# Two-layer trunk on one core: x parked in DRAM to give the weight ring a sixth place, shared-expert units spread over more blocks, and the second layer's gate and MoE conditioning summed on VectorE inside the delta rule's heads

## The chip, the cores and the metric

One core of a Trainium2 chip. The metric is device time in microseconds for one launch of the whole kernel; smaller is better. Engine names are those of the profile: PE is TensorE, DVE is VectorE, ACT is ScalarE, POOL is GpSimd, SP is SyncE, whose queue issues the weight loads.

## The reference

Input x is 512 positions by 1024 channels, float32. Two layers run over it. Each layer's six modulation vectors come from a conditioning vector c through a large matrix (`ada_w`, 1024 by 6144 per layer).

```python
cs = silu(c)
for i in range(2):
    mod = cs @ ada_w[i] + ada_b[i]
    sh1, sc1, gt1, sh2, sc2, gt2 = split(mod, 6)
    h = rmsnorm(x, norm_w[i, 0]) * (1 + sc1) + sh1
    y = short_conv_mixer(h, ...) if i == 0 else gated_deltanet_mixer(h, ...)
    x = x + gt1 * rmsnorm(y, norm_w[i, 1])
    h = rmsnorm(x, norm_w[i, 2]) * (1 + sc2) + sh2
    y = hier_moe(h, ...)
    x = x + gt2 * rmsnorm(y, norm_w[i, 3])
```

`short_conv_mixer` is a projection to three times the width, a causal convolution of three taps between two gates, and an output projection. `gated_deltanet_mixer` is linear attention with 8 heads of 128: a projection to q, k, v, z and two small columns (beta and decay) per head, a causal convolution of four taps, then per chunk of positions a triangular solve and a state update, a norm, a gate by z, and an output projection. `hier_moe` routes each of the 512 positions to 2 of 64 experts; each expert is 1024 to 256 (gate and up) and back (down), 3 MB of float32 weights. A shared expert with hidden width 512 runs over all positions.

## The kernel before

The kernel is written for one core, in the order mixer 0, MoE 0, mixer 1 (the delta rule), MoE 1.

**The ring.** All large weights pass through `load()` (lines 121 to 138). It takes a tile of 128 by 4096 floats (2 MB) from a pool of 5 buffers, and issues one DMA (L137) or two halves (L135) on SP's queue. SP's order is the order in which the code calls `load()`; a load waits until the instructions that read the old piece in its buffer are done. x itself lies in SBUF beside the ring, 16 KB of each partition, in the same size as one ring piece. At the end of each MoE x is also in SBUF for the residual addition.

**A MoE stage.** The experts are taken in 18 blocks, 14 of four experts' slots ("Q") and 4 of two ("P"), in the order of the string `ORDER`. A Q block needs four ring pieces of gate and up weights (`block_gu`) and two of down weights (`block_dn`). TensorE's order is written out by hand here: gate and up (L1322, PSUM tile `gu`), gather of the next blocks' rows (L1270), scatter of the block before (L1379, `sca`, added into `y` by VectorE at L1384), the down-projection (L1357, tile `po`; for the last block L1346, tile `pol`). In between come units of the shared expert: eight of `shared_up` (L1408) and four of `shared_down` (L1431), one unit at each Q block from 2 to 15, and two at block 16. Behind the last block's gate and up comes a loop for expert overflow (L1530), which does not run for this input, but in front of which every engine waits for the others and for all DMAs in flight. Then the last block's rows are scattered and, chunk by chunk, `finish_chunk` multiplies by the gate (`ft`, L1681 on VectorE and L1682 on GpSimd) and adds into x (L1686).

**The seam to layer 1.** The norm of the next layer follows (`norm_t`: transposes L333, output `ghi` and `glo`, L343 to L345), together with one group of the modulation.

**Modulation.** `ada_units(i, groups, ...)` makes one of three groups of `ada_w[i]` at a time: group 0 is shift and scale before the mixer, group 1 the mixer's gate and the MoE's shift, group 2 the MoE's scale and its gate. One group is four ring pieces. Two ways exist: `unit` multiplies on TensorE (16 matmul steps per piece, L271), and `unit_summed` forms the weighted sum over the 8 parts of the contraction on VectorE (`adasum`, L286 and L288), so that TensorE needs only a row (L216), four short sums (L292), and the finish (L216 gate, L230 columns). In the kernel before, three groups are summed on VectorE during mixer 0: groups 1 and 2 of layer 0 and group 0 of layer 1. Group 1 of layer 1 is made with `unit` at the seam, and group 2 with `unit` in head 7 of the delta rule.

**The delta rule.** The Tile scheduler sets the order of all engines but SP here. For each head a 2 MB piece `gdn_w` is split into a high and a low part (`whi` on ScalarE, L680, `wlo` on GpSimd, L681, in eighths with four buffers), and three matmuls per part and channel block (L383 to L385, tile `pj`, 96 a head) make q, k, v and z. These stand between the small steps of the head before: the matrix L of the chunk (`LT`), four Newton steps between TensorE and VectorE (`Tc`, `V`, `Uc`; L874 to L894), the larger blocks of the inverse (`W`, `T`, `U`; L906 to L929), and the state steps (`vn`, `S`; L945 to L959). Ahead of head 0 stand two columns per head from a small piece `gdn_ba` (tile `ba`, `beta`, the decay `gg` at L738).

## Time and profile before

| | us |
|---|---|
| runs of the kernel before | 1823.75, 1824.9, 1825.8; median 1824.9 |
| profiled execution, its own time | 1825.65 |
| its span on the device | 1823.8 |
| TensorE busy | 1616.1 (89%) |
| VectorE busy | 852.8 (47%) |
| ScalarE busy | 479.1 (26%) |
| GpSimd busy | 175.6 (10%) |
| HBM read | 517.11 MB, 286 GB/s over the span |

The stages lie in the span about as follows: mixer 0 until 204 us, output projection and the front of MoE 0 until 268, MoE 0 until 786, the seam until 830, the delta rule until 1233, output projection and front until 1283, MoE 1 until 1801, the last additions and stores until the end. The share of TensorE is an average over stages whose limits differ, so the tables by stage and the timeline at the seams say more than the page.

### The profile page before, as it was taken

To read this page: it belongs to the slowest core of one execution; us is meant where nothing else is said; L and a number is where in the kernel's file an instruction comes from. 1 tells how busy PE (TensorE), PEld (TensorE's weight loads), DVE (VectorE), ACT (ScalarE), POOL (GpSimd) and SP (SyncE) were. 2 spreads that over 40 slices of the span, in tenths; PEclk is the share of its full clock that TensorE was granted. 3 is DMA by queue.
4 is the path that set the end of the run, shared out by engine and by line. 5 is a ranking of instruction groups with operands and counts; after the bars stand their busy time and mean duration, and the time that the engine had idled before them with its cause. 6 is when DMAs were issued, how large, how long until landed. Compare 5 with 4: busy or idle time off the path is not lost. (4 is left out here: it accounts for less than half of the span.)

```text
span 1823.8 us, 27772 instructions
## 1 busy us (share of the span) xinstructions
PE 1616.1 (89%) x11102; PEld 985.6 (54%) x11102; DVE 852.8 (47%) x1761; ACT 479.1 (26%) x978; POOL 175.6 (10%) x160
## 2 busy tenths in 40 slices
PE   6999977899999998868998999998689999989985
PEld 3777755445445454426676766656444545445542
DVE  1886454434334342445666666625543424334335
ACT  4222351211111110034344434415231111111101
POOL 1000110000000000024323323310000000000001
PEclk8999987999999999988999999999699999999997
DMA  9873426999999999786111111116589999999992
GB/s 402 353 304 124 202 108 250 376 419 418 420 417 411 419 419 419 292 353 244 62 59 59 59 59 59 53 59 271 208 336 420 416 419 418 419 419 415 420 399 93
DMA packets 71511, 523.17 MB, mean 287 GB/s; under 512 B 8340, under 2 KB 8532, under 8 KB 16852
## 3 DMA queue, kind: packets, MB, share of 16 engines
q1 hardware_dynamic: 67684, 511.02, 68.6%
q10 hardware_dynamic: 3696, 10.34, 1.6%
q8 instruction: 89, 1.46, 0.3%
q14 instruction: 42, 0.34, 0.0%
HBM read 517.11 MB, written 4.23 MB: 286 GB/s over the span
## 5 line engine op out<-in xcount | busy, mean ns | idle before, releaser
L1384 DVE TENSOR_TENSOR y<-y,sca 128x512 f32<-128x512 f32 x272 | 186.0, 686 | 97.3 <-PE sca L1379 96.4
L1322 PE MATMUL gu<-ring,xTb 128*32 128x512 f32 (+1 forms) x1024 | 170.6, 634 | 31.8 <-DMA ring<-in_moe_gu 31.8
L1270 PE MATMUL gat<-ohg,ghi 128*128 128x256 f32 x576 | 162.6, 304 | 32.1 <-DVE ohg L1245 10.8
L1326 DVE TENSOR_TENSOR hid<-hid,gu 128x256 f32<-128x256 f32 x36 | 15.2, 421 | 311.0 <-ACT hid L1325 311.0
L1270 PE MATMUL gat<-ohg,glo 128*128 128x256 f32 x576 | 154.7, 291 | 0.0
L1270 PEld LDWEIGHTS gat<-ohg,ghi 128*128 128x128 f32 x576 | 113.8, 198 | 61.4 <-ACT xTb L1276 17.4
L1379 PE MATMUL sca<-ohi,G 128*128 128x512 f32 x288 | 126.4, 439 | 15.6 <-DVE y L1382 5.4
L1322 PE MATMUL gu<-ring,xTa 128*32 128x512 f32 (+1 forms) x1024 | 134.6, 610 | 0.2
L1322 PEld LDWEIGHTS gu<-ring,xTb 128*32 128x32 f32 (+1 forms) x1024 | 47.3, 119 | 147.1 <-issue 82.9
L1379 PE MATMUL sca<-olo,G 128*128 128x512 f32 x288 | 118.5, 411 | 0.0
L1270 PEld LDWEIGHTS gat<-ohg,glo 128*128 128x128 f32 x576 | 114.1, 198 | 7.9
L1357 PE MATMUL po<-ring,hT 128*32 128x512 f32 (+1 forms) x896 | 118.1, 602 | 0.0
L1682 POOL TENSOR_TENSOR ft<-y,gt 128x512 f32<-128x512 f32 x8 | 12.4, 1550 | 1058.9 <-DVE y L1384 1058.1
L1408 PE MATMUL mix<-h2T,shw 128*128 128x512 f32 x256 | 114.1, 599 | 0.0
L385 PE MATMUL pj<-ghi,wlo 128*128 128x512 f32 x264 | 113.4, 430 | 0.2 <-POOL wlo L681 0.2
L383 PE MATMUL pj<-ghi,whi 128*128 128x512 f32 x264 | 110.3, 418 | 1.6 <-DVE xh L789 0.8
L1325 ACT ACTIVATE hid<-gu 128x256 f32<-128x256 f32 x36 | 13.9, 385 | 357.8 <-PE gu L1322 357.8
L384 PE MATMUL pj<-glo,whi 128*128 128x512 f32 x264 | 107.8, 408 | 0.0
L681 POOL TENSOR_TENSOR wlo<-ring,whi 128x512 fp32r<-128x512 f32 x66 | 86.1, 1305 | 184.7 <-ACT whi L680 125.1
L1372 DVE SCALAR_TENSOR_TENSOR olo<-po,tab_s,ohi 128x512 fp32r<-128x512 f32 x68 | 51.1, 751 | 96.6 <-ACT ohi L1371 96.6
L1379 PEld LDWEIGHTS sca<-ohi,G 128*128 128x128 f32 x288 | 56.1, 195 | 62.8 <-issue 31.1
L1322 PEld LDWEIGHTS gu<-ring,xTa 128*32 128x32 f32 (+1 forms) x1024 | 36.6, 115 | 88.5 <-issue 88.2
(402 smaller groups left out, 2781.7 us busy)
## 6 DMA issues: line engine op xcount, KB each, us to landing
ring<-in_moe_gu SPq DMA_DIRECT2D x256, 1024.0 KB, 14.5
ring<-in_moe_w_down SPq DMA_DIRECT2D x120, 1024.0 KB, 13.2
ring<-in_ada_w SPq DMA_DIRECT2D x24, 2048.0 KB, 10.8
ring<-in_gdn_w SPq DMA_DIRECT2D x8, 2048.0 KB, 12.3
ring<-in_conv_in_w SPq DMA_DIRECT2D x8, 1536.0 KB, 11.8
shw<-in_shared_gu SPq DMA_DIRECT2D x16, 512.0 KB, 15.4
x<-in_x SPq DMA_DIRECT2D x8, 512.0 KB, 6.3
ring<-in_conv_out_w SPq DMA_DIRECT2D x2, 2048.0 KB
```

The source lines that it names most:

```text
L383: mm(out, ah, bh, start=first, stop=False)
L384: mm(out, ah, bl, start=False, stop=False)
L385: mm(out, al, bh, start=False, stop=last)
L681: nc.gpsimd.tensor_tensor(out=wlo, in0=w[:, k:k + 4], in1=r32(whi), op=ALU.subtract)
L1270: nc.tensor.matmul(g[:, kk], part[:, c, k], oh[:, c], start=(kk + c + lo == 0), stop=(kk + lo == 2 and c == TC - 1), skip_group_check=True)
L1322: nc.tensor.matmul(gu[s * j:s * j + s], xT[k][:, s * j:s * j + s], pieces(j, k), start=(k == 0), stop=(k == K - 1), skip_group_check=True)
L1326: nc.vector.tensor_tensor(out=hid, in0=hid, in1=gu[:, 256:512], op=ALU.mult)
L1357: self.nc.tensor.matmul(po[h][s * j:s * j + s], hT[:, k, s * j:s * j + s], pieces(j, k)[:, 512 * h:512 * h + 512], start=(k == 0), stop=(k ...
L1372: nc.vector.scalar_tensor_tensor(lo, po[h], gcol, r32(hi), op0=ALU.mult, op1=ALU.subtract)
L1379: nc.tensor.matmul(sc, G[:, c * P:(c + 1) * P], part, start=(n == 0), stop=(n == 1))
L1384: nc.vector.tensor_tensor(out=ys, in0=ys, in1=sc, op=ALU.add)
L1408: nc.tensor.matmul(acc, w[:, k], self.h2T[:, k], start=(k == 0), stop=(k == K - 1))
```

## The change

1. **Ring.** The pool of 5 buffers becomes a list of 5 named tiles, `self.pieces`, taken round robin (`ring_63` to `ring_67` in the listings below). At the start of a MoE stage x's own tile is appended to the list as a sixth place. For that, each chunk of x is written to a DRAM tile `xk` on ScalarE's queue as soon as the output projection has added into it. Behind the last block's weights, SP reads the four chunks back into x, ahead of the overflow loop.
2. **Units.** The table `UNITS` names the block of each of the 12 shared-expert units: 2, 3, 5, 5, 6, 8, 9, 9, 11, 12, 14, 15. Block 16 has none, and the gate rows move from block 16 to 15.
3. **Modulation.** Groups 1 and 2 of layer 1 are no longer made with `unit`, but summed on VectorE as 16 half-units (one 128x2048 operation each), two in each head of the program text. Their partial sum, rows and copy live in one ring piece that the list gives up (`held`), so the ring has four places during the delta rule. The next layer's norm now takes eight PSUM tiles at once. The second half of the output weights is loaded after the loop over k instead of before it.

```diff
+UNITS = (2, 3, 5, 5, 6, 8, 9, 9, 11, 12, 14, 15)
...
-            t = self.ring.tile([P, 4096], F32, name="ring")
+            t = self.pieces.pop(0)
+            self.pieces.append(t)
...
+            self.pieces = [ring.tile([P, 4096], F32, name="ring%d" % n) for n in range(5)]
...
+            self.xk = tc.dram_tile([T, D], F32, name="xk")
...
-        def unit_summed(g, q):
+        def unit_summed(g, q, kks=range(2)):
...
-            w = self.load(wv[g, q].rearrange("p (k n) -> p k n", k=2), [P, 2, 2048])
-            if q == 0:
-                part[g] = sb.tile([P, 2048], F32, name="adasum", bufs=2)
-            for kk in range(2):
+            if 0 in kks:
+                piece[0] = self.load(wv[g, q].rearrange("p (k n) -> p k n", k=2), [P, 2, 2048])
+            w = piece[0]
+            if q == 0 and 0 in kks:
+                part[g] = kept[0] if kept else sb.tile([P, 2048], F32, name="adasum", bufs=2)
+            for kk in kks:
...
+        if kept:
+            return [lambda g=g, q=q, kk=kk: unit_summed(g, q, [kk]) for g in groups for q in range(4) for kk in range(2)]
...
+                if front:
+                    nc.scalar.dma_start(out=self.xk[c * P:(c + 1) * P], in_=self.x[:, c])
...
+                if not self.only:
+                    held = self.pieces.pop(0)
+                    kept = held[:, :2048], held[:, 2048:2560], held[:, 2560:3072]
+                    units = self.ada_units(1, [1, 2], sb, ps2, ("ob", 1, "ob", 1), summed=True, kept=kept)
...
+                    units[2 * h]()
...
-                        if h == H - 1 and not self.only:
-                            if n == 0:
-                                wo = [self.load_out(A["gdn_out_w"], 0)]
-                                units = self.ada_units(1, [2], sb, ps2, ("ob", 1, "ob", 1, "kt", 2, "xh", 2))
-                            units[n]()
+                        if h == H - 1 and not self.only and n == 0:
+                            wo = [self.load_out(A["gdn_out_w"], 0)]
...
+                    units[2 * h + 1]()
...
+            if not self.only:
+                self.xplace = self.x.rearrange("p c d -> p (c d)")
+                self.pieces.append(self.xplace)
...
-                for f in self.ada_units(1, [1], sb, ps, ("gat", 1, "gat", 1, "", 0, "olo", 2), hs[:, 0]):
-                    f()
...
-            n = 2 if b == NB - 2 else int(ne == 4 and not last and b > 1)
+            n = UNITS.count(b)
...
-            if b == NB - 2:
+            if b == NB - 3:
                 gt = self.gate_rows(shw, ps, 1, ("shw", "mix"))
...
+        if not self.only:
+            self.pieces = [p for p in self.pieces if p is not self.xplace]
+            for c in range(TC):
+                nc.sync.dma_start(out=self.x[:, c], in_=self.xk[c * P:(c + 1) * P])
         po = self.down_last(ps, hT, ne, dn)
         self.overflow(i, m, rt, hs, sb, ps)
-        if i == 0 and not self.only:
-            nc.scalar.dma_start(out=hs[:, 0], in_=self.A["rows"][1])
```

Where the scheduler sets the order, the diff does not show what moves. Three places, each before and after. A row is an instruction in its engine's order: line, operation, output and input tiles, size, and in brackets the engines or DMA lanes on which it waits.

TensorE at the seam, the end of the next layer's norm before (`np` are its transposes, `adaacc`, `adagp` and `adacp` are group 1, `pj` the projection):

```order
L333 MATMUL np<-cst,h2T 128x128 [waits DVE_49]
L333 MATMUL np<-cst,h2T 128x128 x3
L271 MATMUL adaacc<-ring,cs 32x512 [waits DMAHW1_49]
L271 MATMUL adaacc<-ring,cs 32x512 x7
L216 MATMUL adagp<-hs,cst 128x512 [waits Activation_49]
L230 MATMUL adacp<-cst,md 64x2 [waits DVE_49]
L230 MATMUL adacp<-cst,md 64x2 x15
L383 MATMUL pj<-ghi,whi 128x512 [waits DVE_49,Activation_49,Pool_49]
```

The same place now:

```order
L345 MATMUL np<-cst,h2T 128x128 [waits Activation_49]
L345 MATMUL np<-cst,h2T 128x128 x4
L345 MATMUL npo<-cst,h2T 128x128 x2
L345 MATMUL np<-cst,h2T 128x128
L395 MATMUL pj<-ghi,whi 128x512 [waits DVE_49,Activation_49,Pool_49]
L396 MATMUL pj<-glo,whi 128x512
```

The weight matmuls, the gate and the columns have left; the projection follows the last transpose.

SP's queue from the end of MoE 0 on, before (`gdn_w` are the heads' projection weights, `ada_w` the modulation's):

```order
L137 DMA ring<-in_gdn_ba 128x1024
L137 DMA ring<-in_ada_w 128x4096 x3
L137 DMA ring<-in_ada_w 128x4096 [waits DMAHW1_49]
L137 DMA ring<-in_gdn_w 128x4096 [waits DMAHW3_49,PE_49]
L137 DMA ring<-in_gdn_w 128x4096 [waits DMAHW4_49,PE_49]
```

And now:

```order
L141 DMA ring_63<-in_gdn_ba 128x1024
L141 DMA ring_65<-in_gdn_w 128x4096
L141 DMA ring_66<-in_ada_w 128x4096
L141 DMA ring_67<-in_gdn_w 128x4096
L141 DMA ring_63<-in_ada_w 128x4096 [waits DMAHW2_49,Pool_49]
L141 DMA ring_65<-in_gdn_w 128x4096 [waits DMAHW5_49,DMAHW3_49,Pool_49]
L141 DMA ring_66<-in_ada_w 128x4096 [waits DMAHW4_49,DMAHW3_49,DVE_49]
L141 DMA ring_67<-in_gdn_w 128x4096 [waits DMAHW7_49,DMAHW5_49,Pool_49]
```

Pieces of `ada_w` and `gdn_w` alternate through all eight heads, over four places; a piece waits for GpSimd's split of an older `gdn_w` piece, or for VectorE's sum of an older `ada_w` piece.

VectorE in head 3's Newton steps, before:

```order
L872 TENSOR_TENSOR Uc<-Uc,gcst 128x128 [waits DVE_49]
L970 TENSOR_SCALAR so<-so 128x4 [waits DVE_49]
L843 TENSOR_TENSOR DT<-gr,gcst 128x512 [waits DMAHW5_49]
L874 STREAM_TRANSPOSE Tc<-Uc 128x128 [waits DVE_49]
L972 TENSOR_TENSOR so<-so,cf 128x4 [waits Pool_49]
L881 TENSOR_TENSOR V_7800<-iv,gcst 128x128 [waits PE_49]
```

And now (`ring_64` is the held piece with the partial sum):

```order
L894 TENSOR_TENSOR Uc<-Uc,gcst 128x128 [waits DVE_49]
L296 TENSOR_SCALAR ring_64<-ring_66,cs 128x2048 [waits DMAHW2_49,PE_49]
L896 STREAM_TRANSPOSE Tc<-Uc 128x128 [waits DVE_49]
L988 TENSOR_TENSOR so<-cf 128x4 [waits Activation_49]
L298 SCALAR_TENSOR_TENSOR ring_64<-ring_66,cs,ring_64 128x2048 [waits DVE_49]
L903 TENSOR_TENSOR V_7635<-iv,gcst 128x128 [waits PE_49]
```

The first two half-units of group 2 stand in the first Newton step, ahead of `Tc` and ahead of `V`; two more stand in the next one. On TensorE 57 `pj` matmuls stand between head 3's first and last Newton step where 28 stood before, and 69 instead of 48 stand ahead of the matmuls on the decay `gg`. Of the 16 half-units the scheduler puts two ahead of the norm's output, two around the copy `ba`, two ahead of head 0's L, two in head 0's last steps, four in head 3's Newton steps, two where head 3 passes to head 4, and two in head 4's last steps.

## Rows read from the trace of the kernel before

**Rows 1.** Engine busy by stretch: window; us; PE, PEld, DVE, ACT, POOL (count); PEclk, DMA share, GB/s

```profile
276.00:293.00 17.00, 13.00 (x66) 8.75 (x70) 6.88 (x28) 2.04 (x4) 0.00 (x0) 0.61 0.31 130
340.00:785.00 445.00, 409.21 (x2359) 207.13 (x2352) 157.18 (x281) 66.55 (x126) 0.00 (x0) 0.98 0.97 400
430.00:700.00 270.00, 254.27 (x1481) 129.67 (x1474) 99.12 (x173) 44.09 (x84) 0.00 (x0) 0.99 1.01 417
755.00:785.00 30.00, 24.28 (x142) 10.58 (x141) 7.32 (x13) 1.96 (x4) 0.00 (x0) 1.00 0.39 159
765.00:775.00 10.00, 9.33 (x54) 3.65 (x56) 5.14 (x8) 0.60 (x1) 0.00 (x0) 1.00 0.00 1
1770.00:1800.00 30.00, 24.77 (x132) 10.52 (x133) 7.46 (x13) 1.96 (x4) 0.00 (x0) 0.89 0.39 155
935.00:978.00 43.00, 40.07 (x488) 30.65 (x488) 28.20 (x76) 18.32 (x53) 14.49 (x12) 1.00 0.18 62
```

**Rows 2.** TensorE's groups by line, 340 to 785 and 1340 to 1801: busy, mean | idle before, releaser

```profile
L1322 PE MATMUL gu<-ring,xTb 128*32 128x512 f32 (+1 forms) x448 | 79.8, 659 | 15.6 <-DMA ring<-in_moe_gu 15.6
...
L1322 PE MATMUL gu<-ring,xTb 128*32 128x512 f32 (+1 forms) x448 | 76.3, 620 | 16.2 <-DMA ring<-in_moe_gu 16.2
```

**Rows 3.** TensorE's timeline, ends of both MoE stages: start, duration, operation [idle before <-releaser]

```profile
748.39 3.72 PE L1431 MATMUL sda<-shw,hs 128*128 128x256 f32 x16 [0.97 <-DVE y L1435]
...
782.17 3.62 PE L1346 MATMUL pol<-ring,hT 128*32 128x512 f32 x26 [0.99 <-DMA ring<-in_moe_w_down]
...
1797.54 3.62 PE L1346 MATMUL pol<-ring,hT 128*32 128x512 f32 x26 [0.92 <-DMA ring<-in_moe_w_down]
```

**Rows 4.** VectorE's timeline at the seam and ahead of head 0

```profile
794.83 0.69 DVE L1384 TENSOR_TENSOR y<-y,sca 128x512 f32<-128x512 f32 x1 [5.54 <-PE sca L1379]
...
840.49 0.23 DVE L715 COPY ba<-tp 128x64 f32<-128x64 f32 x1 [3.90 <-PE tp L712]
...
845.81 1.15 DVE L738 SCALAR_TENSOR_TENSOR gg<-xa,ea 128x32 f32<-128x32 f32 x1
```

**Rows 5.** TensorE's timeline, the projection's first matmul and two later ones

```profile
830.63 0.77 PE L383 MATMUL pj<-ghi,whi 128*128 128x512 f32 x1 [0.78 <-ACT whi L680]
...
842.12 0.40 PE L383 MATMUL pj<-ghi,whi 128*128 128x512 f32 x1
842.36 0.39 PE L384 MATMUL pj<-glo,whi 128*128 128x512 f32 x1
```

**Rows 6.** The tile adasum, its operations in mixer 0: count, duration in ns min/median/max

```profile
L288 DVE SCALAR_TENSOR_TENSOR adasum<-ring,cs,adasum x21: 2342/2349/2353, 50.3 to 152.1; 128x2048 f32<-128x2048 f32 x21
L286 DVE TENSOR_SCALAR adasum<-ring,cs x3: 1274/1282/1283, 49.0 to 120.3; 128x2048 f32<-128x2048 f32 x3
```

**Rows 7.** The page's DMA issues: count, KB each, us from issue to landing

```profile
ring<-in_gdn_w SPq DMA_DIRECT2D x8, 2048.0 KB, 12.3
```

**Rows 8.** GpSimd's timeline in head 0, the last eighth of a split

```profile
889.19 1.29 POOL L681 TENSOR_TENSOR wlo<-ring,whi 128x512 fp32r<-128x512 f32 x1 [3.32 <-PE pj L385]
```

**Rows 9.** VectorE's timeline in head 0's last steps

```profile
899.53 0.28 DVE L917 TENSOR_SCALAR T<-iv 32x128 f32<-32x128 f32 x1
...
904.85 0.35 DVE L950 TENSOR_SCALAR vn<-sc,cf 128x128 f32<-128x128 f32 x1 [0.95 <-PE sc L945]
```

**Rows 10.** TensorE's timeline, the finish of a summed group in mixer 0

```profile
156.58 1.12 PE L216 MATMUL adaacc<-rows,cst 4*128 4x512 f32 x2
157.63 1.06 PE L292 MATMUL adaacc<-adasum,cst 128*32 128x512 f32 x8
...
159.73 2.09 PE L230 MATMUL adacp<-cst,md 128*64 128x2 f32 x32
```

**Rows 11.** TensorE's groups by line in head 7, 1181 to 1199

```profile
L271 PE MATMUL adaacc<-ring,cs 128*32 128x512 f32 x64 | 10.7, 656 | 0.0
```

**Rows 12.** VectorE's timeline at the seam, the residual addition beside GpSimd's work and alone

```profile
802.87 2.32 DVE L1686 SCALAR_TENSOR_TENSOR x<-ft,fst,x 128x1024 f32<-128x1024 f32 x1
...
811.38 1.27 DVE L1686 SCALAR_TENSOR_TENSOR x<-ft,fst,x 128x1024 f32<-128x1024 f32 x1
```

More of the change, by code (lines that the diff above doesn't have):

```diff
@@ L41 @@
 NB = len(ORDER)
+UNITS = (2, 3, 5, 5, 6, 8, 9, 9, 11, 12, 14, 15)
+assert all(ORDER[b] == "Q" for b in UNITS)
 def block_ranks():
@@ L142, in run @@
         with tc.tile_pool(name="glob", bufs=1) as glob, \
-                tc.tile_pool(name="ring", bufs=5) as ring, \
+                tc.tile_pool(name="ring", bufs=1) as ring, \
                 tc.manual_schedule(engines={mybir.EngineType.SP}):
-            self.glob, self.ring = glob, ring
+            self.glob = glob
+            self.pieces = [ring.tile([P, 4096], F32, name="ring%d" % n) for n in range(5)]
             self.cst = glob.tile([P, C_END], F32, name="cst")
@@ L205, in ada_units @@
     def ada_units(self, i, groups, sb, ps, tags=("adaacc", 1, "adagp", 1, "adarow", 1, "adamd", 1),
-                  rows=None, queue=None, summed=False):
+                  queue=None, summed=False, kept=None):
         nc, A, m = self.nc, self.A, self.mods[i]
         wv = A["ada_w"][i]
-        if rows is None:
-            rows = sb.tile([P, 512], F32, tag=tags[4], name="rows", bufs=tags[5])
-            (queue or nc.scalar).dma_start(out=rows, in_=A["rows"][i])
+        rows = kept[1] if kept else sb.tile([P, 512], F32, tag=tags[4], name="rows", bufs=tags[5])
+        (queue or nc.scalar).dma_start(out=rows, in_=A["rows"][i])
         def row(g, acc, start):
@@ L219, in done @@
         def done(g, acc):
-            md = sb.tile([P, 512], F32, tag=tags[6], name="md", bufs=tags[7])
+            md = kept[2] if kept else sb.tile([P, 512], F32, tag=tags[6], name="md", bufs=tags[7])
             nc.scalar.activation(md, acc, AF.Copy)
@@ L288, in unit_summed @@
                     nc.vector.scalar_tensor_tensor(part[g], w[:, kk], c, part[g], op0=ALU.mult, op1=ALU.add)
-            if q == 3:
+            if q == 3 and 1 in kks:
                 place(g)
@@ L295, in unit_summed @@
                 done(g, acc[g])
-        part = {}
+        part, piece = {}, [None]
+        if kept:
+            return [lambda g=g, q=q, kk=kk: unit_summed(g, q, [kk]) for g in groups for q in range(4) for kk in range(2)]
         return [lambda g=g, q=q: (unit_summed if summed else unit)(g, q) for g in groups for q in range(4)]
@@ L767, in mixer1 @@
                 neg = gcst[:, C_NEG:C_NEG + P][:, None, :].to_broadcast([P, TC, P])
+                units = [lambda: None] * 16
+                if not self.only:
+                    held = self.pieces.pop(0)
+                    kept = held[:, :2048], held[:, 2048:2560], held[:, 2560:3072]
+                    units = self.ada_units(1, [1, 2], sb, ps2, ("ob", 1, "ob", 1), summed=True, kept=kept)
                 Uf = [sb.tile([P, TC, P], F32, name="U%d" % n) for n in range(2)]
@@ L982, in mixer1 @@
                     wo = [self.load_out(A["gdn_out_w"], 0)]
-                wo.append(self.load_out(A["gdn_out_w"], 1))
+                else:
+                    self.pieces.append(held)
                 sums = {c: ps.tile([P, T], F32, tag=("pj", "pj", "tp", "gq")[c], name="oacc", bufs=2 if c < 2 else 1)
@@ L994, in mixer1 @@
                         self.mm3(sums[c], yhi[:, c, k], ylo[:, c, k], whi, wlo, k == 0, k == K - 1)
+                wo.append(self.load_out(A["gdn_out_w"], 1))
             self.project_out(A["gdn_out_w"], 1, begun=(wo, sums))
@@ L1502, in moe @@
                 m1 = self.mods[1]
-                place = ["gu", "gu", "sca", "sca", "mix"]
+                place = ["gu", "gu", "sca", "sca", "mix", "", "", "gat"]
                 po = ps.tile([P, 2, T], F32, tag="po", name="npo", bufs=1)
@@ L1508, in tile_ps @@
                         return po[:, k - 5]
-                    tag = place[k % 7]
-                    return ps.tile([P, T], F32, tag=tag, name="np", bufs=1 if tag == "mix" else 2)
+                    return ps.tile([P, T], F32, tag=place[k], name="np", bufs=2 if k < 4 else 1)
                 self.wba = self.load_ba()
-                self.norm_t(self.xn, tile_ps, lambda k: self.y[:, k // 2, T * (k % 2):T * (k % 2) + T], m1)
-                for f in self.ada_units(1, [1], sb, ps, ("gat", 1, "gat", 1, "", 0, "olo", 2), hs[:, 0]):
-                    f()
+                self.norm_t(self.xn, tile_ps, lambda k: self.y[:, k // 2, T * (k % 2):T * (k % 2) + T], m1, K)
             self.xsrc = self.xs
```

## Prediction

> **What bounds the kernel now.** I read the page first, then tables by stage, then the timeline at the seams. In the two MoE stages the 16 DMA engines are the wall: from 430 to 700 us their share is 1.01 at 417 GB/s [rows 1], and TensorE, busy 254 of those 270 us, loses its time in front of the ring: the second gate/up matmuls stood idle 15.6 us in layer 0 and 16.2 us in layer 1 until a load landed [rows 2]. The granted clock over the stage averages 0.98 [rows 1], which over its 445 us is some 9 us more, most of it right behind such waits. But the stream of weights has two holes. Before block 0 gives back its first piece, 276 to 293, the share is 0.31: all five places are full, and 11.7 us of DMA lie idle. At the end, from 755 to 785, the share is 0.39, 11.7 us of transfer, with ten us of 0.00 in the middle, 765 to 775, before the last pieces move [rows 1]. The reason stands in TensorE's timeline: places come free as it consumes pieces, and at that time it works through four half downs of the shared expert, each 3.72 us with 0.97 of waiting in front, 18.8 us in all, and the gate rows [rows 3].
>
> In the delta rule it is the reverse: in one head (43 us) TensorE is busy 40.07 us, VectorE 28.20, GpSimd 14.49, and DMA has a share of 0.18 [rows 1]. Bytes are free there, and VectorE has 14.8 us a head, in small gaps.
>
> **The sum** is made against the profiled execution's own 1825.65 us, 0.75 above the median of the three runs.
>
> **MoE, layer 0.** By transfers: the sixth place holds 2.1 MB, at 417 GB/s 5.0 us, and is filled in the idle 11.7 us before 293. The 11.7 us of transfer that are left at 755 then end at 755 + 11.7 - 5.0 = 761.7, if no place is held. The spread sees to that: the 18.8 us of downs and the gate rows leave the end. Behind the weights x is read back, another 5.0 us, and the overflow loop's barrier waits for it: 766.7, and some 2 us of landing (my estimate from the 12.3 us of a flight [rows 7] against 2 x 5.0 of transfer), 768.7. The last down-projection (3.62 us behind its final piece [rows 3]) ends near 767, beside it. Before, it ended at 782.17 + 3.62 = 785.8. Gain 17.1. By TensorE: the waits of 15.6 and 0.99 us [rows 2, 3] and the clock's 9 are 25; the early blocks keep some 5 of it, because the moved units come only later, so 20. I take the smaller, 17, since the DMA is the wall. The write of x to DRAM (2.1 MB, 5.0 us) is issued while the output projection ends, and I cost it at nothing: its cover is the hole before 293. If it displaces a fill there, it costs its 5.0.
>
> **MoE, layer 1.** The same shape: 0.39 of 1770 to 1800 [rows 1], 1770 + 11.7 - 5.0 + 5.0 + 2 = 1783.7 against a last projection that ended at 1797.54 + 3.62 = 1801.2 [rows 3]. Gain 17.
>
> **Transition.** Removed: TensorE's matmul of the rows stood between the scatters and waited for its DMA, so that VectorE's next addition came 5.54 us late [rows 4]; then 64 weight matmuls between the norm's transposes. The projection's first matmul is at 830.63, behind that group's columns [rows 5]; in the new order it stands right behind the last transpose. Against this VectorE gets four half-units here, 1.28 + 3 x 2.35 = 8.3 us [rows 6], two before the norm's output and two around the copy for beta, ahead of which it now waits 3.90 us for TensorE [rows 4]; most fits, but the second piece must have landed. The decay is ready at 846.96 now [rows 4]; I expect it 5 us earlier, and TensorE by then 21 projection matmuls further (4.9 us, since they start 0.24 apart at most [rows 5]). Of these 10 I book **-7**, between -3 and -10.
>
> **Heads.** Added on VectorE: 12 half-units, one of 1.28 and eleven of 2.35, 27.1 us [rows 6]. What leaks to TensorE is their length less VectorE's idle time at that place and less the matmuls that TensorE has beside them, since the two hand the chain to and fro and TensorE's order is fixed. Two ops before head 0's first L: 27 more projection matmuls stand there (6.3 us), leak 0. Two in head 0's last steps: 4.7 less gaps of 0.95 at most [rows 9] and of some 0.6, leak 3.1. Four in head 3's Newton steps, 8.3 us: 57 projection matmuls stand there against 28, 6.8 us more cover, 1.5 left; the stretch behind is that much barer: 2. Two at the border to head 4 and two in head 4: 3.2 and 3.1. Together **+11**, with 0 and 27.1 as ends. Finishing a group (row, four sums, gate, columns) costs TensorE 1.12 + 1.06 + 1.12 + 2.09 = 5.4 us [rows 10]; group 1's now falls in head 3: **+5.4**. Head 7 loses 64 weight matmuls, 10.7 us [rows 11], keeps a finish, and has output projection matmuls as cover in its Newton steps: **-10**. Heads +6.4; with the transition -0.6.
>
> On SP each ada piece now stands behind a gdn_w piece, which waits for GpSimd's split of an earlier one. I cost that at nothing; its cover is the DMA share of 0.18. The split's last eighth in head 0 starts at 889.19 and takes 1.29 [rows 8], 9 us before the T operation at 899.53 [rows 9], right behind which the next ada piece is wanted; a flight is 12.3 us [rows 7], 3 too long. But GpSimd may split as far ahead as TensorE's projection matmuls allow, and the new order has 10 to 25 more of them done at the same step, so the piece is there some us ahead.
>
> **Where a rule speaks against it.** The residual addition at the transition took 2.32 us while GpSimd multiplied and 1.27 alone [rows 12]; the sums in layer 0 took 2.35 each with GpSimd idle [rows 6], and now they stand beside its 14.49 us a head. The price from these rows: 1.05 us for an op that meets one of GpSimd's, 11.6 us if all eleven do, 3.9 by GpSimd's share of 34%. My sum has 0 of it; with the 3.9 it would be 1794. The Trainium skill, "SBUF — State Buffer", section "Who interferes with whom", says that a VectorE instruction with two SBUF inputs contends with a GpSimd instruction that reads SBUF, and that whichever is issued first has the shared ports for its whole length. By that rule, the trace agrees with 2.32 against 1.27.
>
> **Sum:** -17 - 17 - 0.6 = -34.6, rounded to -35: 1825.65 - 35 = **1790.5**.
>
> **The rivals.**
> 1. *VectorE leaks whole.* All 27.1 us land on TensorE, 16 more than in my sum, and collisions with GpSimd take the 3.9: **1810.5**. For: VectorE's gaps inside the chain are under 1 us [rows 9]. Against: it idles a third of a head, and TensorE's order has matmuls put beside most of the ops.
> 2. *x's traffic eats its place.* Write and read are 10 us of DMA a layer; if the write displaces a fill and the read stands between the last weight and the barrier, 10 of each 17 are lost: **1810.5**. For: the share of 1.01 in between. Against: the two holes [rows 1].
> 3. *Slower: the sums wait for their pieces.* VectorE works in order; an op put ahead of its piece's landing stops the whole chain behind it. Six pieces are used in the heads; at 35 / 6 = 5.9 us each it decides. At two thirds of a flight, 8.2 us, it is 49: **1839.5**. For: the 9 us against 12.3 above, and a ring of four places. Against: the projection further ahead, and DMA's rest.
> 4. *The place is never early.* If x's place is free only when block 0 returns others, the moved units merely shift the waits, and what is left pays for the leak: no change, **1825**.
>
> A better case: TensorE's 20 in both layers and no leak, -20 - 20 - 7 - 4.6, **1774**.
>
> **How the numbers follow.** Forecast 0.58; rival 1 0.14, rival 2 0.13, rival 3 0.08, rival 4 0.03, the better case 0.04. The forecast's own range, with 12 to 20 a layer and a leak of 0 to 20, is 1774 to 1806. The range of 8 in 10 takes in rivals 1 and 2 as sized and leaves out 3, 4 and the far ends: **1772 to 1811**. Faster by over 0.2% (3.65 us, about what a measurement of this kernel can tell from no change): 0.58 + 0.14 + 0.13 + 0.04 = 0.89; same 0.03; slower 0.08.
>
> **What would show it.** Right: no ten us with a share of 0.00 before the last weights; the ring's waits down to a few us a layer; the last down-projections near 768 and, in layer 1, 17 us nearer to the stage's start; additions behind the barrier without the 5.54; heads of 43 to 47 us in which TensorE's waits for VectorE grew by some 11 in all; head 7 some 10 shorter. Wrong: sums whose idle time before them was ended by a DMA (rival 3); sums of 3 us and more (the ports, rival 1); a barrier that waits for x, or as much waiting for the ring as before (rivals 2 and 4).

## The result, and the profile after

The changed kernel took a median of 1795.28 us (1792.42 to 1797.45, four runs) against 1825.35 of the kernel before on the same chip: ratio 0.9836, interval 0.9819 to 0.9853. The profiled execution took 1795.03 us, with a span of 1793.2, so 30.6 us of span are gone where the sum had 35.

Where they went shows at five points of the two timelines: the first `ohi` behind the barrier of each MoE stage, the decay `gg`, the first `LT` of head 0, and the last `oacc` of the output projection's first half.

| stretch (us) | before | after | difference | forecast |
|---|---|---|---|---|
| start to the barrier of MoE 0 | 786.53 | 767.50 | -19.0 | -17.1 |
| barrier to the end of `gg` | 60.4 | 58.2 | -2.2 | -7 (the decay 5 earlier, 2 for TensorE's lead) |
| `gg` to head 0's `LT` | 27.4 | 39.6 | +12.2 | 0 |
| `LT` to the last `oacc` | 358.8 | 356.7 | -2.1 | +6.4 |
| `oacc` to the barrier of MoE 1 | 568.4 | 548.1 | -20.3 | -17 |
| barrier to the end | 22.3 | 23.1 | +0.8 | 0 |

The MoE stages gave somewhat more than forecast, the seam less, and head 0 lost what no term of the sum had. Head 0's first `LT` in the kernel before:

```profile
874.34 0.35 DVE L854 SCALAR_TENSOR_TENSOR LT<-gq,cf,DT 128x128 f32<-128x128 f32 x1
```

The windows of after, which answer to [rows 1]:

```profile
276.00:293.00 17.00, 14.91 (x86) 9.76 (x87) 5.14 (x20) 2.04 (x4) 0.00 (x0) 0.71 0.55 218
340.00:765.00 425.00, 398.33 (x2348) 205.08 (x2340) 155.66 (x276) 66.52 (x126) 0.00 (x0) 0.98 1.01 417
755.00:765.00 10.00, 6.58 (x42) 1.50 (x34) 0.42 (x1) 0.77 (x2) 0.00 (x0) 1.00 0.95 377
1760.00:1770.00 10.00, 5.84 (x34) 1.49 (x34) 0.03 (x1) 0.38 (x1) 0.00 (x0) 1.00 0.74 300
935.00:978.00 43.00, 40.21 (x496) 30.98 (x495) 27.73 (x79) 17.77 (x51) 12.34 (x10) 1.00 0.29 111
```

The share (next to last number) before block 0 gives back its pieces rose from 0.31 to 0.55, and from 340 on the DMA engines run at 1.01 to the stage's end: in layer 0 the ten us of 0.00 have become 0.95, and the last ten of layer 1 stand at 0.74. In front of the second gate/up matmuls the waits for the ring fell by 12 us a layer, from [rows 2] to these two groups (340 to 765 and 1320 to 1765):

```profile
L1344 PE MATMUL gu<-ring,xTb 128*32 128x512 f32 (+1 forms) x416 | 56.0, 611 | 3.9 <-DMA ring<-in_moe_gu 3.9
...
L1344 PE MATMUL gu<-ring,xTb 128*32 128x512 f32 (+1 forms) x448 | 59.7, 608 | 4.2 <-DMA ring<-in_moe_gu 4.2
```

The ends of both stages on TensorE, and ScalarE's first operation behind each barrier, for [rows 3]:

```profile
761.69 3.62 PE L1368 MATMUL pol<-ring,hT 128*32 128x512 f32 x26 [1.70 <-DMA ring<-in_moe_w_down]
...
1764.25 3.62 PE L1368 MATMUL pol<-ring,hT 128*32 128x512 f32 x26 [1.47 <-DMA ring<-in_moe_w_down]
...
767.50 1.27 ACT L1393 ACTIVATE ohi<-pol,tab_s 128x512 fp32r<-128x512 f32 x2 [9.96 <-DMA x<-xk]
...
1770.09 1.27 ACT L1393 ACTIVATE ohi<-pol,tab_s 128x512 fp32r<-128x512 f32 x2 [9.08 <-DMA x<-xk]
```

The last down-projection ends at 765.31 and 1767.87, and each barrier opens 2.2 us later, released by the read of x; before it opened 0.7 and 0.3 us behind the last down-projection (786.53 and 1801.50).

### The profile page after: what moved, and what is told of

Its sections match the earlier page's. It is cut to its first block, busy times and chain, and to the rows that moved or that the text cites. A ratio compares the mean times of both kernels' runs of the same rounds, so it can differ in the third digit from the quotient of the medians.

```text
span 1793.2 us, 27730 instructions
## 1 busy us (share of the span) xinstructions
PE 1592.0 (89%) x10990; PEld 987.3 (55%) x10990; DVE 882.0 (49%) x1777; ACT 476.8 (27%) x978; POOL 186.9 (10%) x160
## 4 chain that ended last, share of the span: by engine, by line
PE 35%; DVE 8%; DMA 5%; ACT 3%; POOL 2%; issue 2%; ACTq 0%; SPq 0%; POOLq 0%; DVEq 0%
PE gu L1344 6%; PE gat L1292 4%; PE sca L1401 3%; PE po L1379 3%; PE mix L1430 2%; DMA ring<-in_moe_gu 2%; PE pj L396 2%; PE pj L397 2%; PE pj L395 2%; PE sda L1453 2%; DMA ring<-in_moe_w_down 1%; POOL rr L847 1%; DMA x<-xk 1%; DVE xh L810 1%; POOL wlo L695 1%
## 5 line engine op out<-in xcount | busy, mean ns | idle before, releaser
L1292 PE MATMUL gat<-ohg,ghi 128*128 128x256 f32 x576 | 162.5, 304 | 31.9 <-ACT xTa L1298 10.6
L1344 PE MATMUL gu<-ring,xTa 128*32 128x512 f32 (+1 forms) x736 | 138.8, 629 | 0.2
L1344 PE MATMUL gu<-ring,xTb 128*32 128x512 f32 (+1 forms) x960 | 126.6, 608 | 8.1 <-DMA ring<-in_moe_gu 8.1
L395 PE MATMUL pj<-ghi,whi 128*128 128x512 f32 x264 | 114.1, 432 | 6.8 <-ACT y L351 6.8
L695 POOL TENSOR_TENSOR wlo<-ring,whi 128x512 fp32r<-128x512 f32 x66 | 92.4, 1402 | 207.6 <-ACT whi L694 172.4
L1344 PEld LDWEIGHTS gu<-ring,xTb 128*32 128x32 f32 (+1 forms) x960 | 36.5, 114 | 91.2 <-issue 73.9
```

What stands on the lines that cost most here:

```text
L395: mm(out, ah, bh, start=first, stop=False)
L695: nc.gpsimd.tensor_tensor(out=wlo, in0=w[:, k:k + 4], in1=r32(whi), op=ALU.subtract)
L1292: nc.tensor.matmul(g[:, kk], part[:, c, k], oh[:, c], start=(kk + c + lo == 0), stop=(kk + lo == 2 and c == TC - 1), skip_group_check=True)
L1344: nc.tensor.matmul(gu[s * j:s * j + s], xT[k][:, s * j:s * j + s], pieces(j, k), start=(k == 0), stop=(k == K - 1), skip_group_check=True)
```

## The experiments

Runs whose labels share a letter ran in one group on one chip; before's median was 1825.55 in a, 1821.43 in b, 1825.75 in c and 1824.56 in d.

### a1: the changed kernel without the place

```diff
-            self.xk = tc.dram_tile([T, D], F32, name="xk")
...
-                if front:
-                    nc.scalar.dma_start(out=self.xk[c * P:(c + 1) * P], in_=self.x[:, c])
...
-                self.pieces.append(self.xplace)
...
-                nc.sync.dma_start(out=self.x[:, c], in_=self.xk[c * P:(c + 1) * P])
```

> The changed kernel without the sixth place: x is neither written to DRAM nor read back, the ring has five places in the MoE stages; units stay spread, modulation stays on VectorE in the heads. Theory A (the spread of the units frees the end of each MoE stage, the place gives its own 5.0 us of early fill less some 1.5 us that the barrier now waits for x): 3.5 to 5 us a layer slower than the changed kernel, about 1803 (1800 to 1806). Rival B (the sixth place is what took the waits of 31.8 us for the ring away): 10 us a layer or more, 1815 or more, with the ring's waits back at 20 us or more.

Measured: 2088.18 us, ratio 1.1442 [1.1417, 1.1468]. This says nothing on the price of the place. A Q block loads six pieces, and with five named tiles the sixth load, a down piece, falls on the tile of the first gate/up piece ahead of that one's reading in program order. So the gate/up matmuls wait for and multiply by down weights. TensorE's groups of this kernel, 430 to 700, show it:

```profile
L1341 PE MATMUL gu<-ring,xTa 128*32 128x512 f32 (+1 forms) x208 | 45.2, 765 | 50.0 <-DMA ring<-in_moe_w_down 50.0
```

What follows: a list of tiles taken round robin must be as long as what one block loads before it reads its first piece. Place and spread had to be told apart from the other side (a2, b1, b2).

### a2, b1, b2: place and spread apart

a2 is the changed kernel with the old order of the units:

```diff
-UNITS = (2, 3, 5, 5, 6, 8, 9, 9, 11, 12, 14, 15)
+UNITS = (2, 3, 5, 6, 8, 9, 11, 12, 14, 15, 16, 16)
...
-            if b == NB - 3:
+            if b == NB - 2:
```

> The changed kernel with the units at the blocks of before (two downs and the gate rows at block 16), sixth place kept. Theory A: the 18.8 us of downs sit again between the last pieces and the places they need; 11 to 14 us a layer slower than the changed kernel, about 1820 (1815 to 1824), with a stretch of DMA share 0 again before the last pieces. Rival B: the place covers the hole, at most 5 us a layer, 1805 or less.

Measured: 1808.85 us (1808.13 to 1813.75), ratio 0.9911 [0.9889, 0.9934]: between the two expectations, nearer to B.

b1 is the kernel before with the spread alone:

```diff
-            n = 2 if b == NB - 2 else int(ne == 4 and not last and b > 1)
+            n = UNITS.count(b)
...
-            if b == NB - 2:
+            if b == NB - 3:
```

> The kernel before with nothing but the table of units and the gate rows at block 15; ring of five buffers, x stays, modulation as before. Theory A (the units fill the waits for the ring and leave the end; the place gives its early 5.0 us less the 1.5 us of the barrier): most of the MoE gain of some 36 us is there, 1825 - 28 = 1797 (1792 to 1802). Rival B (unit table and place only work together: with five places the last pieces are still held): 1810 or more.

Measured: 1810.95 us (1808.87 to 1814.11), ratio 0.9932 [0.9914, 0.995]. Theory A, 1797, is out.

A first kernel with list, place and spread but without the moved modulation, a3, was laid out wrongly: the second half of the output weights, loaded ahead of the loop over k, falls as sixth load on the tile of the first half before that is read, so that the second mixer's output projection multiplies by the wrong half of its weights.

```diff
+            self.pieces = [ring.tile([P, 4096], F32, name="ring%d" % n) for n in range(5)]
...
+                self.pieces.append(self.xplace)
...
+            n = UNITS.count(b)
```

> The kernel before with sixth place and spread units only; the second layer's modulation as before (TensorE at the seam and in head 7). Theory A (from the traces: the seam and the delta rule together became 5.7 us longer by the change): 6 us faster than the changed kernel, about 1789 (1786 to 1792). Rival C (the modulation on VectorE pays as forecast or better, -0.6 or up to -7): 1795 to 1802.

Measured: 1800.89 us, 1793.24 to 1809.18, ratio 0.9853 [0.9823, 0.9884]; too scattered to weigh against the changed kernel. b2 is the same with that load behind the loop:

```diff
-                wo.append(self.load_out(A["gdn_out_w"], 1))
...
+                wo.append(self.load_out(A["gdn_out_w"], 1))
```

> The kernel before with the sixth place and the table of units; the second layer's modulation on TensorE as before. Only the second half of the output weights is loaded behind the loop over k, as in the changed kernel. Theory A (seam and delta rule became 5.7 us longer by the modulation's move): 1789 (1786 to 1792). Rival C (the move pays): 1796 or more.

Measured: 1795.26 us (1792.26 to 1796.95), ratio 0.9844 [0.9825, 0.9864]. Theory A, 1789, is out. The changed kernel ran beside it once more:

> The changed kernel itself, beside the others on one chip: 1795 (1792 to 1798) against 1825 of the kernel before.

Measured: 1794.7 us (1793.23 to 1795.16), ratio 0.9844 [0.9825, 0.9863].

The same group of MoE 0 in a2, b1 and b2 (340 to 785), and the two windows of a2 that answer to [rows 1]:

```profile
L1344 PE MATMUL gu<-ring,xTb 128*32 128x512 f32 (+1 forms) x416 | 66.4, 611 | 13.4 <-DMA ring<-in_moe_gu 13.4
```

```profile
L1325 PE MATMUL gu<-ring,xTb 128*32 128x512 f32 (+1 forms) x448 | 69.9, 610 | 10.5 <-DMA ring<-in_moe_gu 10.3
```

```profile
L1332 PE MATMUL gu<-ring,xTb 128*32 128x512 f32 (+1 forms) x416 | 57.0, 608 | 4.9 <-DMA ring<-in_moe_gu 4.9
```

```profile
276.00:293.00 17.00, 13.33 (x71) 8.37 (x72) 6.54 (x25) 2.04 (x4) 0.00 (x0) 0.66 0.59 245
765.00:775.00 10.00, 8.57 (x82) 2.59 (x78) 0.42 (x1) 0.77 (x2) 0.00 (x0) 1.00 0.65 237
```

What follows: with one of the two alone most of these waits for the ring stay; with both they go to 4.9. The place without the spread (a2) fills the early idle time, 0.59 for 0.31, but the end of the stage keeps a share of 0.65. The barrier of MoE 0 opens at 780.6 with the spread, at 776.6 with the place and at 768.9 with both, against 786.5: -5.9, -9.9 and -17.6, so the parts nearly add up, and the place is the larger. (Six kernels with the same code up to this barrier open it between 765.2 and 769.6 in their traces, so each part is good to some 2 us.) By medians of one chip, spread and then place: 1821.43, 1810.95, 1795.26, some 10 and 16 us over two layers.

b2 and b4 are equal. So the moved modulation, with everything that hangs on it, paid nothing here. The next runs ask why.

### a4: the sums shortened

Fourteen of the sixteen half-units sum 8 of their 2048 columns; the rest of the modulation's sum is left out.

```diff
-                else:
+                elif not kept:
...
+                else:
+                    nc.vector.scalar_tensor_tensor(part[g][:, :8], w[:, kk, :8], c, part[g][:, :8], op0=ALU.mult, op1=ALU.add)
```

> The changed kernel in which 14 of the 16 half-units of groups 1 and 2 of layer 1 sum 8 of 2048 columns only (the rest of the sum is left out); loads, rows and finishes stay. The scheduler moves a few rows of the heads. Theory A (the length of the sums on VectorE, and GpSimd's ops that they hold up, is the cost): heads and seam together 15 to 20 us shorter, 1775 to 1781. Rival D (the cost is DMA: pieces that land late, or small transfers of head 0 held up by the 4 MB of gdn_w and ada_w behind the same instant): at most 8 us, 1787 or more.

Measured: 1784.89 us (1784.01 to 1786.19), ratio 0.9775 [0.9747, 0.9802], 10.4 below the changed kernel's median, between the two expectations, though some 30 us of sums went away (33.8 in after, 3.9 left). By the timeline the gain lies ahead of the heads: barrier to the end of `gg` 6.5 us shorter, from there to head 0's first `LT` another 12.2, while `LT` to the last `oacc` took 8.5 longer than in after. So the seam and head 0 are where the shorter sums saved time. What the sums cost in the heads, a4 does not tell cleanly: its order there is another (from head 3's `LT` to head 4's it took 53.3 us, after 47.8), and by head 0's first `LT` TensorE had begun 131 projection matmuls where after had begun 162. And a4 also changed a second thing there, which led to the next run: the decay came early enough to be written and read back before the next weights were issued.

### b3: the decay's round trip ahead of the weights

In head 0 the decay is written to DRAM (`gd`, four small transfers) and read back in another layout (`gr`). In after, the write was issued at 830.97 on ScalarE's queue, and right behind it SP issued 4 MB of weights. ScalarE's and SP's timelines, then VectorE's:

```profile
830.97 3.40 ACTq L775 DMA_DIRECT2D gd<-th  x4
842.24 0.34 ACTq L796 DMA_DIRECT2D gr<-gd  x1
842.63 0.63 ACT L812 ACTIVATE th<-xh 128x512 f32<-128x512 f32 x1 [7.53 <-DMA gd<-th]
...
831.52 0.33 SPq L141 DMA_DIRECT2D ring<-in_gdn_w  x1
831.95 0.55 SPq L141 DMA_DIRECT2D ring<-in_ada_w  x1
...
847.17 0.69 DVE L865 TENSOR_TENSOR DT<-gr,gcst 128x512 f32<-128x512 f32 x1 [3.19 <-DMA gr<-gd]
```

From the issue of the write to that of the read passed 11.3 us, from the write to `DT` 16.2. In the kernel before these were 6.2 and 10.0, and its next weights were issued only behind the read:

```profile
849.75 3.40 ACTq L761 DMA_DIRECT2D gd<-th  x4
855.96 0.34 ACTq L775 DMA_DIRECT2D gr<-gd  x1
...
857.82 0.33 SPq L137 DMA_DIRECT2D ring<-in_gdn_w  x1
...
859.71 1.42 DVE L843 TENSOR_TENSOR DT<-gr,gcst 128x512 f32<-128x512 f32 x1 [0.71 <-DMA gr<-gd]
```

On the same queue a4 had 6.2 and 9.9, and issued its next weights at 832.08, behind its read at 830.20. The test puts both small transfers of head 0 on SP's queue, ahead of those weights, for which the first two pieces of each kind are taken earlier in the program text:

```diff
+                    for h in range(2):
+                        early.append(self.load(A["gdn_w"][h].rearrange("p (k n) -> p k n", k=K), [P, K, 512]))
+                        kept[3].append(self.load(A["ada_w"][1][1, h].rearrange("p (k n) -> p k n", k=2), [P, 2, 2048]))
...
-                    nc.scalar.dma_start(out=gd[:, :, c], in_=gro[H * c:H * c + H])
+                    nc.sync.dma_start(out=gd[:, :, c], in_=gro[H * c:H * c + H])
...
-                    nc.scalar.dma_start(out=gr.rearrange("p n c t -> p (n c t)"),
+                    (nc.scalar if h else nc.sync).dma_start(out=gr.rearrange("p n c t -> p (n c t)"),
```

> The changed kernel, with the decay's write to DRAM and head 0's read of it put on SP's queue ahead of the third gdn_w piece and the ada_w piece behind it, so that they do not wait for 4 MB of weights. Theory E (in head 0 that write was issued 0.5 us ahead of the 4 MB, came back after 11.3 us where before it took 6.2, and ScalarE stood for it): the first L of head 0 4 to 6 us earlier, 1790.5 (1789 to 1792). Rival F (VectorE's two sums there set the end of that stretch anyway): at most 1.5 us, 1793.5 or more.

Measured: 1784.18 us (1779.17 to 1789.74), ratio 0.9797 [0.9775, 0.9818], against 1794.7 of the changed kernel beside it: 10.5 us, about twice what theory E expected. SP's and VectorE's timelines of b3:

```profile
828.78 3.00 SPq L784 DMA_DIRECT2D gd<-th  x4
832.97 0.34 SPq L803 DMA_DIRECT2D gr<-gd  x1
833.43 0.35 SPq L141 DMA_DIRECT2D ring<-in_gdn_w  x1
833.83 0.42 SPq L141 DMA_DIRECT2D ring<-in_ada_w  x1
...
837.81 0.69 DVE L872 TENSOR_TENSOR DT<-gr,gcst 128x512 f32<-128x512 f32 x1 [0.27 <-DMA gr<-gd]
848.38 0.35 DVE L883 SCALAR_TENSOR_TENSOR LT<-gq,cf,DT 128x128 f32<-128x128 f32 x1
```

What follows: write to `DT` is 9.0 us, `gg` to `DT` 14.3 instead of 21.4, and head 0's `LT` comes 24.9 us behind `gg` instead of 39.6. That weights issued beside the round trip delay it is shown, by a4 on ScalarE's queue and by b3 on SP's; its share of the 10.5 is not quite, since the scheduler also put the two sums that stood ahead of head 0's `LT` behind it. In after's own timeline the two are told apart: `gg` to `DT` grew from 12.8 to 21.4 us, +8.7, and `DT` to `LT` from 14.6 to 18.2, +3.5. Of the 8.7, 2.5 arise before the write is issued (5.2 us from `gg` to the write instead of 2.8; b3 keeps 5.3) and 6.2 from the write to `DT`. For the second part, VectorE's and GpSimd's timelines of after:

```profile
855.36 2.34 DVE L298 SCALAR_TENSOR_TENSOR ring<-ring,cs,ring 128x2048 f32<-128x2048 f32 x1
857.62 1.29 DVE L844 TENSOR_SCALAR s<-s 128x4 f32<-128x4 f32 x1
858.82 2.34 DVE L298 SCALAR_TENSOR_TENSOR ring<-ring,cs,ring 128x2048 f32<-128x2048 f32 x1
862.07 0.18 DVE L848 RECIPROCAL rr<-rr 128x4 f32<-128x4 f32 x1 [0.91 <-POOL rr L847]
865.32 0.34 DVE L876 SCALAR_TENSOR_TENSOR LT<-gq,cf,DT 128x128 f32<-128x128 f32 x1
...
856.04 2.85 POOL L695 TENSOR_TENSOR wlo<-ring,whi 128x512 fp32r<-128x512 f32 x1 [1.68 <-ACT whi L694]
858.99 3.05 POOL L847 TENSOR_TENSOR rr<-s,tok 128x4 f32<-128x4 f32 x1
```

The first sum stands ahead of `s`, and GpSimd's small `rr`, on which `LT` hangs, took 3.05 us beside the second one, where its median is 1.008.

### c2: the same round trip without the moved sums

b2 with the decay ahead of the weights, the first four `gdn_w` pieces taken early:

```diff
+                early = [] if self.only else [self.load(A["gdn_w"][h].rearrange("p (k n) -> p k n", k=K), [P, K, 512])
+                                              for h in range(4)]
...
-                    nc.scalar.dma_start(out=gd[:, :, c], in_=gro[H * c:H * c + H])
+                    nc.sync.dma_start(out=gd[:, :, c], in_=gro[H * c:H * c + H])
```

> The kernel with sixth place and spread units only (b2, modulation on TensorE at the seam and in head 7), and the decay's write and head 0's read put on SP's queue ahead of the fifth gdn_w piece. It tells what the modulation's move is worth where nothing collides in head 0: theory I (the move pays some 6 us, as 435 us from the barrier to the last head in b3 against 441 before): 1790 (1788 to 1793), 6 us slower than b3. Rival J (the move pays nothing; b3 gained only by its write): 1784 or less.

Measured: 1788.85 us (1787.26 to 1793.36), ratio 0.9802 [0.9786, 0.9817]. b2 had its own form of the delay: `gd` issued at 832.87 and `DT` at 845.71, 12.8 us. So c2 is faster than b2 by 6.4 us at the median of the same chip (7.7 by the ratios), from `gg` to head 0's `LT` it took 33.6 us instead of 37.9, and against b3 its ratio is the same. Its time lies where theory I had it, but its distance to b3 does not decide between the two. What the moved modulation pays by itself once the decay is out of the way is not settled: 4.7 us by the medians of b3 and c2, nothing by their ratios.

### c1, d1, d2: x read back behind the overflow loop

c1 takes b3 and moves the read of x from ahead of the overflow loop to behind it:

```diff
-            for c in range(TC):
-                nc.sync.dma_start(out=self.x[:, c], in_=self.xk[c * P:(c + 1) * P])
         po = self.down_last(ps, hT, ne, dn)
         self.overflow(i, m, rt, hs, sb, ps)
+        if not self.only:
+            for c in range(TC):
+                nc.sync.dma_start(out=self.x[:, c], in_=self.xk[c * P:(c + 1) * P])
```

> The kernel with the decay's write first (b3), and x read back behind the overflow loop instead of ahead of it. Theory G (ScalarE's first operation behind the barrier came 2.2 us after the last projection in layer 0 and 4.8 us after it in layer 1, where it was 0.7 and 0.3 before the change, because the barrier waits for x; x itself is wanted 6 us later): 5 to 6 us faster than b3, 1784 - 5.5 = 1778.5 (1776 to 1781). Rival H (x then lands late for the first residual addition, and the next weights behind it): no faster than b3, 1783 or more.

Measured: 1779.04 us (1777.38 to 1780.8), ratio 0.9738 [0.9725, 0.9751].

> c1 again, beside d1 on one chip, so that the two can be compared: 1779 (1777 to 1782) by both theories, 46 us faster than the kernel before.

Measured: 1779.97 us (1774.82 to 1785.48), ratio 0.9757 [0.9731, 0.9783]. This is the fastest version found, about 15 us below the changed kernel. How much of it the later read gives is open: the medians are 5.1 and 4.2 below b3's, and c1's interval lies below b3's, but b3's runs scatter over 10.6 us, and the profiled spans are 1777.2 (b3), 1779.0 (c1) and 1773.0 (d2). At the barriers the traces show less than theory G counted on: ScalarE's first operation follows the last down-projection by 0.3 us in both layers of c1 and d2, by 1.8 and 2.2 in b3, so 3.3 us were to be had; the 4.8 of the expectation is 2.2 in the traces of after and b3. d1 makes c1's edit in c2, to weigh the moved modulation a second time:

> c2 (modulation on TensorE, decay's write first) with x read back behind the overflow loop, as in c1: the two differ only by the modulation's move. Theory I (the move pays 5 to 7 us once head 0 is undisturbed: 441.7 us from the barrier to the last output projection matmul in b3 against 448.7 in c2): 5 to 7 us slower than c1 on the same chip, 1785 (1783 to 1787). Rival J (the move pays nothing): within 2 us of c1.

Measured: 1796.18 us (1792.86 to 1799.75), ratio 0.9841 [0.9816, 0.9865], on the chip of d2 and 16.2 us above it, where neither theory had it. It does not weigh the modulation alone: d1 is slower than c2 too, by 7.3 us at the medians of two chips. SP's and TensorE's timelines of c2, then of d1:

```profile
766.00 4.31 SPq L141 DMA_DIRECT2D ring<-in_ada_w  x4
...
804.80 2.09 PE L238 MATMUL adacp<-cst,md 128*64 128x2 f32 x32 [1.58 <-DVE gr L249]
```

```profile
765.08 3.04 SPq L1672 DMA_DIRECT2D x<-xk  x4
768.17 0.43 SPq L141 DMA_DIRECT2D ring<-in_gdn_ba  x1
768.64 6.71 SPq L141 DMA_DIRECT2D ring<-in_ada_w  x4
...
807.90 2.09 PE L238 MATMUL adacp<-cst,md 128*64 128x2 f32 x32 [0.77 <-DVE gr L249]
```

x's four chunks now stand on SP ahead of the seam's four `ada_w` pieces, and the group's columns come 3.1 us later. Barrier to last `oacc` took 460.2 us in d1 and 448.7 in c2. Of these 11.5 us, 2.6 lie between the barrier and the end of `gg`, where the columns' delay stands, and 2.9 between there and head 0's `LT`, whose cause is open. The other 6.0 have little to do with the read: up to head 7's `LT` the heads took 301.4 us in d1 and 301.3 in c2, and behind it the same 558 matmuls ran at a granted clock of 0.83 in d1 and 0.94 in c2 (third number from the end):

```profile
1166.32:1225.71 59.39, 56.43 (x558) 35.94 (x556) 18.91 (x58) 12.16 (x38) 9.66 (x8) 0.83 0.16 58
...
1161.24:1214.73 53.49, 50.56 (x558) 32.03 (x556) 18.91 (x58) 12.14 (x38) 9.66 (x8) 0.94 0.18 63
```

So the late read is seen to delay the seam where the seam has weights to load, by some 3 us in this one pair of traces, and the worth of the moved modulation stays between 0 and some 5 us.

## Why the prediction was right, and where it was not

The forecast of 1790.5 was 4.8 us too low. The side, the likeliest mechanism and the range held. The parts were sized less well than the sum: the two MoE stages gave 5.2 us more than booked, and everything between them 8.5 less. That these nearly meet is luck.

**MoE 0.** Forecast: last down-projection near 767, barrier at 768.7, gain 17.1. Measured: 765.31, 767.50, 19.0. The argument by transfers was right, and so was the landing of x, whose wait is 2.2 us. The split inside it was wrong: the place was booked with its one early fill, 5.0 us, and the spread with the rest. b1 and a2 show 5.9 for the spread and 9.9 for the place, each alone.

**MoE 1.** Forecast -17, measured -20.3, with 12.0 us less of waiting for the ring. The figure "by TensorE", 20, set aside as the upper of two, was the better one here.

**x's traffic.** The write cost nothing that shows, as booked: the share stays 1.01 from 340 on. Rival 2 did not happen. Its barrier wait did, but with 2.2 us, of which 0.7 and 0.3 were there before.

**Transition.** Forecast -7, between -3 and -10, of it 5 for the decay; the decay came 2.2 earlier. TensorE's lead came as forecast, 69 projection matmuls begun by the end of `gg` instead of 48; it shows only in the heads. What was removed went as described: the projection stands at 801.46, 34.0 us behind the barrier where it had been 44.1 [rows 5], and `ba` is copied 28.2 us earlier than in [rows 4], 9.2 of it gained since the barrier. The step that failed is "most fits". VectorE's timeline of after, from the copy to the decay:

```profile
812.28 0.22 DVE L729 COPY ba<-tp 128x64 f32<-128x64 f32 x1
812.42 3.25 DVE L298 SCALAR_TENSOR_TENSOR ring<-ring,cs,ring 128x2048 f32<-128x2048 f32 x1
815.59 1.26 DVE L732 TENSOR_SCALAR beta<-beta 128x32 f32<-128x32 f32 x1
...
817.16 1.00 DVE L738 SCALAR_TENSOR_TENSOR ex<-xa 128x32 f32<-128x32 f32 x1
...
819.06 1.30 DVE L742 TENSOR_TENSOR s__5744<-s__5744,ex 128x32 f32<-128x32 f32 x1
820.39 1.22 DVE L743 TENSOR_TENSOR z__5745<-s__5744 128x32 f32<-128x32 f32 x1
...
825.54 0.19 DVE L752 SCALAR_TENSOR_TENSOR gg<-xa,ea 128x32 f32<-128x32 f32 x1
```

From the copy to the end of `gg` passed 13.4 us, against 6.5 before (840.49 to 846.96). One sum of 3.25 lies in it, four small operations that took 0.17 to 0.19 each before take 1.00 to 1.30, and three of 0.75 on head 0's columns came in between. The four ran while GpSimd was splitting weights (810.70 to 818.11 and 819.02 to 821.56). Two of them before:

```profile
840.98 0.19 DVE L724 SCALAR_TENSOR_TENSOR ex<-xa 128x32 f32<-128x32 f32 x1
...
842.11 0.19 DVE L728 TENSOR_TENSOR s__5917<-s__5917,ex 128x32 f32<-128x32 f32 x1
```

Here the price fell on a chain with no cover: TensorE was already past `ba`, and the decay is what head 0 waits for.

**Head 0.** "Leak 0", because 27 more projection matmuls stood there; measured +12.2. TensorE had them (162 begun by the first `LT` instead of 131), and here it did not matter: the chain was on VectorE, GpSimd and a DMA. Of the 12.2 us, 6.2 belong to the decay's round trip, 2.5 to the steps between `gg` and the write, and 3.5 to two sums and the held `rr`. The step that failed first is the one on SP's queue, costed "at nothing; its cover is the DMA share of 0.18". It looked at whether the new pieces land in time, and they did. It did not ask which small transfer they are issued in front of, or beside.

**Heads.** Forecast +6.4 with head 0's part at 0, measured -2.1 from `LT` on. The finish in head 3 costs TensorE 1.12 + 1.06 + 1.12 + 2.09 as booked, and `LT` to `LT` of head 3 is 47.8 us against 44.2. Head 7's steps are 8.0 shorter up to the last `T` (booked 10). That alone would leave some 0.5 us for the leak. But the -2.1 also holds work done ahead: of the 31 projection matmuls more that TensorE had begun by head 0's `LT`, 21 were won at the seam and 10 while head 0's chain was late. At the 0.24 us of [rows 5] they are 7.4 us (an estimate), and from head 0's `LT` to head 1's it took 37.3 us instead of 42.7. So the leak with all the rest is some 6 to 8 us, where the text had 11; its items, 3.1, 1.5, 2, 3.2 and 3.1, in fact add up to 12.9. This term was over-sized, but by less than the table suggests: a part of what the table gives to the heads is the lead from the seam, and a small part is head 0's loss had back. The granted clock is in the rest too: from `LT` to the last `oacc` it was 0.96 in after and 0.99 before (0.98 in b4). How much of the 6 to 8 the sums themselves leak is open, as a4 has another order. Why TensorE absorbs most of them is argued, not shown: in after's head it is busy 40.21 of 43 us, so a later small step may be covered by matmuls that have to be done anyway.

**Rival 1.** GpSimd lost more by it than VectorE's sums did. All 14 sums, by line and operation over the seam and the heads:

```profile
L298 DVE SCALAR_TENSOR_TENSOR ring<-ring,cs,ring 128x2048 f32<-128x2048 f32 x14 | 33.8, 2411 | 0.0
```

Their mean is 2411 ns against a median of 2349 alone [rows 6], 0.9 us over all, nearly all of it the one sum of 3.25. GpSimd's 66 eighths of splits took 92.4 us, 86.1 before. The Trainium skill, "SBUF — State Buffer", section "Who interferes with whom", says that the order of issue decides which of the two engines blocks the other. By that rule the sum, when it is first, pays nothing and GpSimd pays: the trace agrees with `wlo` at 2.85 and `rr` at 3.05 behind sums of 2.34.

**Rivals 3 and 4.** The 0.0 in that row means that no sum waited for its piece. Rival 3 did not happen in its form; what happened is its neighbour, a chain that waited for its own small transfer beside the pieces. Rival 4 did not happen: the share before 293 rose to 0.55.

## What to carry to other kernels

When bulk loads are moved into a quiet stretch, list every small transfer of that stretch on which a chain hangs, and put the write and the read of it into the queue ahead of the loads; the low DMA share on which the forecast relied (0.18 before, 0.63 at that place after) did not rule the delay out. Work that fills an engine's idle time costs little where another engine has matmuls that it must do anyway, and its full length, or more, where the chain is just starting and has nothing beside it, as in the seam. A stretch that comes out shorter may only have less left to do: count the work that is done at its border, before and after, when a sum is checked stretch by stretch. A place more in a ring and an even consumption of its pieces are two remedies for one bound: here each alone left most of the second gate/up matmuls' waits, and only both brought them down.

## What the runs showed of the hardware that was not expected

- A write of four small transfers and its read back, with two 2 MB loads issued within 1 us of the write's start, took 11.3 us from issue to issue instead of 6.2, though the DMA engines' share from 830 to 850 was only 0.63; with the loads issued behind the read it took 4.2 (b3, SP's queue) and 6.2 (a4, ScalarE's).
- Beside a VectorE sum of 2.34 us, GpSimd's 128x4 operation took 3.05 us instead of 1.008, and its eighth of a split 2.85 instead of 1.28.
- VectorE's operations on 128x32, 0.17 to 0.19 us before, took 1.00 to 1.30 beside GpSimd's splits, so the short operations of a chain can lose more there than a long sum.
